# Masks by rows with a place each, output-projection parts issued one by one, a third weight tile in the masks' place, and later loads in order

## The chip, the cores and the metric

The kernel runs on one core of one Trainium2 chip. Its five engines each run their own instruction stream and meet at semaphores: PE multiplies matrices, ACT does activations and copies, DVE and POOL do elementwise work, SP issues the DMAs. The metric is the device time of one execution in microseconds; each kernel is run several times and the median counts.

## The reference, cut to what matters

One inference step of a two-layer trunk of width 1024, over a prompt of 1024 tokens and a sample of 64 tokens that share the weights. Layer 0 is sparse attention (an indexer picks 256 keys for each query) beside a short gated convolution; layer 1 is a spatial gating unit. Only what layer 0 does between the choice of keys and its output projection matters here:

```python
rel = relu(einsum('bqhd,bsd->bqhs', qi, ki))
score = einsum('bqh,bqhs->bqs', wi, rel)
score = where(adm, score, -inf)                 # causal by chunks of 64
top_val, top_idx = lax.top_k(score, topk)       # ties go to the lower index
logits = einsum('bqgrd,bqkgd->bqgrk', q, k[top_idx], ...) * HEAD_DIM ** -0.5
p = softmax(where(valid, logits, -inf))
o = einsum('bqgrk,bqkgd->bqgrd', p, v[top_idx])
a_out = o * silu(ga)
out = concatenate([a_out, b_out], axis=-1) @ w_out
x = x + gate * out
```

Instead of gathering, the kernel finds a threshold for each query by a binary search and adds a mask to dense logits.

## The kernel before

Prompt and sample are one token axis of 1088 columns. Numbers are float32, and each operand of a large product is held as two parts, a rounded high part and the exact rest; a product is three matmuls: high x high, rest x high, high x rest. The parts of the activations are `ah` and `al`, those of a weight tile `w_hi` (ACT, L249) and `w_lo` (POOL, or DVE where asked, L250). A weight tile `w_raw` is 128 x 1024 numbers; two places alternate for it, and each of `w_hi` and `w_lo` has two as well. `split` (L288) makes high and rest of any tile: a copy on ACT (L289) and a subtraction on DVE or POOL (L290).

A framework scheduler sets the order of instructions on each engine by their dependencies and the order of the code; on PE the attention part keeps the order of the code. All DMAs go through SP's queue in its order. A tile of a pool that takes the place of another waits until the other is done with.

In layer 0, after the scores S, `topk` leaves a threshold T for each query. Then:

- **Masks.** Seven blocks j of 128 queries have key widths of 384, 512, 640, 768, 896, 1024 and 576. `mask(j)` does one block: the sign of score less threshold with its sum (ACT, L619), its square with its sum (ACT, L620, written to `cum`), two small steps that count the ties to admit (`cv`, DVE, L621 and L622), a running count over the row (DVE, L623), the choice (DVE, L624) and a scaling to the mask's size (ACT, L625). `cum` is one tile with two halves, used in turn by even and odd blocks. Masks are written to the tile `bias`. All `mask(j)` are issued ahead of the first 360 steps of filler work (`BEFORE`), and the parts of the queries and of the sample's keys (`queries`, `sample_keys`: `st`, `kc`, `qs`) behind those.
- **Attention.** `attend` walks through slots. A slot transposes probabilities (`p_ps`, split into `pth` on ACT and `ptl` on DVE), issues logits some slots ahead (PE `logit_ps` L662; DVE L663 adds the mask and takes the minimum; ACT L667 exponentiates; POOL L669 normalises), and multiplies probabilities by values (`av` L706). Between these PE takes filler matmuls from the generator `side`: first projection tiles (`pj`, L258 and L275), then, once the convolution and the first heads of the first token piece are there (`halved`), the first two output-projection tiles for that piece (`early_out`, L1089).
- **Output projection.** Tokens are in three pieces of 448, 384 and 256 (`OUT_CHUNKS`), inputs in eight blocks k of 128 (`OUT_KTS`), outputs in eight weight tiles. `out_split(c, k)` makes `ah` and `al` of piece c and block k out of `q` (attention, already multiplied by its gate at L1025) or `bo` (convolution). `early_out` issues those of piece 0 in its steps, with `al` on POOL except for k = 3. Those of pieces 1 and 2 are written behind `attend` and are bound by nothing but their inputs, so the scheduler places them as soon as these are ready. The weight tiles from the third on have places in a pool opened after the attention's, with `w_lo` of the third on POOL and of the others on DVE. The residual x is loaded in three pieces: the first on its own, the other two behind the last weight load (`issue_after`). Then x is updated at L1110 out of the product `op`.

The other two names of the prediction: `corner` is a constant part of the masks, and `ln_g`, `ln_b` are the norm weights of layer 1.

Of the kernel before, what the change touches and what calls it, by code (L numbers as in the profile page):

```python
# [9 lines left out]
F32 = mybir.dt.float32  # L10
# [7 lines left out]
P = 128  # L18
# [17 lines left out]
NCH = 3  # L36
# [67 lines left out]
class Trunk:  # L104
# [130 lines left out]
    def weights(self, src, lo_eng="pool", pair=None):  # L235
# [6 lines left out]
        return self.weight_parts(raw, lo_eng, pair or (pool, n))  # L242

    def weight_parts(self, raw, lo_eng, place):
        nc = self.nc
        pool, n = place
        hi = pool.tile([P, KT, P], F32R, tag=f"whi{n}", name="w_hi")
        lo = pool.tile([P, KT, P], F32R, tag=f"wlo{n}", name="w_lo")
# [39 lines left out]
    def split(self, hi, lo, src, lo_eng=None):  # L288
        self.nc.scalar.activation(hi, src, AF.Copy)  # L289
        (lo_eng or self.nc.vector).tensor_sub(lo, src, hi)  # L290
# [315 lines left out]
    def mask(self, j):  # L606
# [5 lines left out]
        n = SW[j]  # L612
        sl = self.S[:, SOFF[j]:SOFF[j] + n]
        bi = self.bias[:, SOFF[j]:SOFF[j] + n]
        p = slice(COL[j], COL[j] + 1)
        c = self.cv[:, p]
        cum = self.cum[:, j % 2 * SEQ:j % 2 * SEQ + n]
        sums = self.small.tile([P, 4], F32, tag="sm", name="sums", bufs=8)
        A.activation(bi, sl, AF.Sign, scale=self.sgn[:, p], bias=self.T[:, p], accum_out=sums[:, 0:1])  # L619
        A.activation(cum, bi, AF.Square, accum_out=sums[:, 1:2])  # L620
        V.tensor_add(c, sums[:, 0:1], sums[:, 1:2])  # L621
        V.tensor_scalar(c, c, 0.5, self.kneg[:, p], op0=OP.mult, op1=OP.add)  # L622
        V.tensor_tensor_scan(cum, self.ones.to_broadcast([P, n]), cum, c, OP.add, OP.subtract)  # L623
        V.scalar_tensor_tensor(bi, cum, 0.0, bi, op0=OP.is_gt, op1=OP.is_gt)  # L624
        A.activation(bi, bi, AF.Copy, scale=MASK)  # L625
# [18 lines left out]
    def logits(self, it, e, c):  # L644
# [21 lines left out]
        if c == k - 1:  # L666
            nc.scalar.activation(p, p, AF.Exp, scale=-1.0, bias=st[:, c:c + 1], accum_out=st[:, 2:3])  # L667
            nc.vector.reciprocal(st[:, 3:4], st[:, 2:3])  # L668
            nc.gpsimd.tensor_scalar(p, p, st[:, 3:4], 0.5, op0=OP.mult, op1=OP.mult)  # L669
# [23 lines left out]
    def weighted(self, pool, it, js, parts):  # L693
# [92 lines left out]
    def attend(self, pool, through, half):  # L786
# [73 lines left out]
    def layer0(self):  # L860
# [41 lines left out]
        with ExitStack() as es:  # L902
# [5 lines left out]
            self.bias = mid.tile([P, STOT], BF, name="bias")  # L908
            self.corner = mid.tile([P, 256], BF, name="corner")
# [65 lines left out]
            with self.pool("attn", "right") as ap:  # L975
                self.at = 0

                self.cum = ap.tile([P, 2 * TC], BF, tag="ga", name="cum")
# [61 lines left out]

                self.halved = False
                self.p, self.both, self.live, self.last = {}, {}, {}, False
                self.side = chain(tiles(), self.early_out(fetch))
                self.tags = ["pj", "pj", "lg", "lg", "lg"]
                with self.tc.manual_schedule(engines={mybir.EngineType.PE}):
                    for j in range(NSB):
                        self.mask(j)
# [3 lines left out]
                    self.queries(ap, 0)  # L1051
                    self.sample_keys(ap)
# [15 lines left out]
    def out_split(self, c, k):  # L1068
# [291 lines left out]
```

## Time and profile before

| | |
|---|---|
| median of 3 runs (lowest to highest) | 1142.4 us (1141.48 to 1142.86) |
| the profiled execution, whole | 1143.23 us |
| its span (first to last instruction) | 1141.5 us |
| mean granted clock of PE | 0.981 |
| masks begin to end (ACT 381.83, last mask copy) | 381.8 to 418.8 us |
| attention ends (last `av`) | 620.5 us |

In rows of the trace the columns are start, duration, engine, line, operation, written tile <- read tiles, shape; "x5" are five in a row, and in square brackets stand the idle time before and what ended it. In groups the columns are the busy time, the mean in ns, and the idle time before with its releasers. In the tables by stretches they are the stretch, its length, then for PE, PE's weight loads, DVE, ACT and POOL the busy time and the number of instructions, then PE's granted clock (1.00 is full), the share of the DMA engines and GB/s.

### The profile page before, as it was taken

The page shows a single profiled execution, that of the slowest core. Times are in us where ns is not written, and L with a number is a line of the kernel's source. Part 1 is how long each engine was busy: PE and PEld are TensorE (multiplying, and loading weights), DVE is VectorE, ACT ScalarE, POOL GpSimd, SP SyncE. Part 2 cuts the span into 40 slices and gives each one's busy share as a digit, 9 for nine tenths or more (in the row PEclk, how much of TensorE's full clock was granted, in tenths as well). Part 3 has the DMA queues.
Part 4 walks back from the last instruction along what each step waited for, and adds up shares of the span by engine and source line. Part 5 has one row for each costly group of instructions (what it writes and reads, how often), then busy time and mean ns, then how long its engine had stood idle before and what let it go on. Part 6 is the DMA issues. An engine that isn't in the chain of part 4 may idle for free.

```text
span 1141.5 us, 18854 instructions
## 1 busy us (share of the span) xinstructions
PE 1088.0 (95%) x7255; PEld 1049.4 (92%) x7255; DVE 659.1 (58%) x1618; ACT 524.0 (46%) x1002; POOL 465.6 (41%) x482
## 2 busy tenths in 40 slices
PE   4899999999999979999978999999999999999996
PEld 4789689999999979999967899999999999999996
DVE  5711799998888697777785344311194064247134
ACT  5232586856766766676764223512212111235111
POOL 2633223466557555464491246422133201154222
PEclk9999999999999989999978899999999999999999
DMA  9745501211001110000002601011112101131012
GB/s 362 313 158 198 201 29 56 77 56 38 27 31 38 57 38 19 20 20 20 20 19 77 228 1 38 1 57 37 46 57 74 44 31 37 38 111 38 1 66 92
DMA packets 25786, 81.84 MB, mean 72 GB/s; under 512 B 3040, under 2 KB 9440, under 8 KB 23264
## 3 DMA queue, kind: packets, MB, share of 16 engines
q1 hardware_dynamic: 25696, 80.63, 19.9%
q8 instruction: 57, 0.93, 0.3%
q14 instruction: 33, 0.27, 0.1%
HBM read 74.50 MB, written 6.12 MB: 71 GB/s over the span
## 4 chain that ended last, share of the span: by engine, by line
PE 82%; DVE 8%; ACT 4%; DMA 2%; issue 2%; POOL 2%; SPq 0%; POOLq 0%; DVEq 0%; ACTq 0%
PE pj L258 41%; PE op L258 15%; PE pj L275 8%; PE av L706 3%; PE logit_ps L662 3%; PE p_ps L688 3%; PE ada_ps L164 1%; PE sgu_ps L1170 1%; PE score_ps L440 1%; PE first L331 1%; DVE cum L623 1%; DVE al L290 1%; POOL hf L342 1%; PE score_ps L441 1%; DMA w_raw<-in_w 1%
## 5 line engine op out<-in xcount | busy, mean ns | idle before, releaser
L258 PE MATMUL pj<-ah,w_hi 128*128 128x364 f32 (+1 forms) x984 | 326.0, 331 | 1.0 <-ACT w_hi L249 1.0
L258 PE MATMUL pj<-al,w_hi 128*128 128x364 f32 (+1 forms) x984 | 323.8, 329 | 0.0
L258 PE MATMUL pj<-ah,w_lo 128*128 128x364 f32 (+1 forms) x984 | 323.0, 329 | 0.0
L250 POOL TENSOR_TENSOR w_lo<-w_raw,w_hi 128x1024 fp32r<-128x1024 f32 x64 | 159.2, 2489 | 337.9 <-ACT w_hi L249 324.2
L258 PEld LDWEIGHTS pj<-ah,w_hi 128*128 128x128 f32 x984 | 185.0, 188 | 2.0 <-ACT w_hi L249 1.3
L258 PEld LDWEIGHTS pj<-ah,w_lo 128*128 128x128 f32 x984 | 184.9, 188 | 0.3 <-issue 0.2
L258 PEld LDWEIGHTS pj<-al,w_hi 128*128 128x128 f32 x984 | 185.1, 188 | 0.0
L258 PE MATMUL op<-ah,w_hi 128*128 128x384 f32 (+2 forms) x368 | 122.2, 332 | 4.3 <-ACT w_hi L249 4.3
L249 ACT ACTIVATE w_hi<-w_raw 128x1024 fp32r<-128x1024 f32 x69 | 73.0, 1059 | 114.3 <-PE pj L258 86.9
L258 PE MATMUL op<-ah,w_lo 128*128 128x384 f32 (+2 forms) x368 | 120.6, 330 | 1.5 <-DVE w_lo L250 1.5
L258 PE MATMUL op<-al,w_hi 128*128 128x384 f32 (+2 forms) x368 | 121.5, 330 | 0.3 <-DVE al L290 0.3
L542 DVE TENSOR_SCALAR_CACHE_REDUCE junk<-S,cand 128x512 bf16<-128x512 f32 (+5 forms) x142 | 119.0, 838 | 1.9
L275 PE MATMUL pj<-ah,w_lo 128*128 128x364 f32 (+1 forms) x288 | 95.8, 332 | 0.9 <-POOL w_lo L250 0.9
L275 PE MATMUL pj<-ah,w_hi 128*128 128x364 f32 (+1 forms) x288 | 95.5, 332 | 0.0
L275 PE MATMUL pj<-al,w_hi 128*128 128x364 f32 (+1 forms) x288 | 95.3, 331 | 0.0
L1110 DVE SCALAR_TENSOR_TENSOR x<-op,mod,x 128x192 f32<-128x192 f32 (+2 forms) x64 | 30.3, 497 | 105.8 <-PE op L258 102.6
L569 ACT ACTIVATE junk<-S,cand 128x896 bf16<-128x896 f32 (+2 forms) x78 | 77.8, 998 | 29.1 <-DVE m L572 25.4
L669 POOL TENSOR_SCALAR S<-S,sm 128x128 f32<-128x128 f32 (+8 forms) x68 | 51.9, 767 | 72.3 <-DVE sm L668 59.7
L258 PEld LDWEIGHTS op<-ah,w_hi 128*128 128x128 f32 x368 | 70.5, 192 | 6.9 <-ACT w_hi L249 5.0
L1118 POOL TENSOR_TENSOR acc<-acc,sq 128x448 f32<-128x448 f32 (+2 forms) x40 | 39.5, 988 | 88.5 <-ACT sq L1116 87.8
L258 PEld LDWEIGHTS op<-ah,w_lo 128*128 128x128 f32 x368 | 70.2, 191 | 4.1 <-DVE w_lo L250 2.1
L258 PEld LDWEIGHTS op<-al,w_hi 128*128 128x128 f32 x368 | 70.4, 191 | 2.6 <-DVE al L290 0.7
(248 smaller groups left out, 2033.8 us busy)
## 6 DMA issues: line engine op xcount, KB each, us to landing
w_raw<-in_w SPq DMA_DIRECT2D x53, 512.0 KB, 3.5
ada<-in_ada_w SPq DMA_DIRECT2D x19, 1024.0 KB, 9.1
w_raw<-in_wo SPq DMA_DIRECT2D x16, 512.0 KB, 3.5
x<-in_x SPq DMA_DIRECT2D x8, 544.0 KB, 6.6
bo<-in_ada_w SPq DMA_DIRECT2D x4, 1024.0 KB, 6.9
x<-in_x SPq DMA_DIRECT2D x1, 1792.0 KB, 8.7
out_y<-x SPq DMA_DIRECT2D x1, 1792.0 KB, 6.6
x<-in_x SPq DMA_DIRECT2D x1, 1536.0 KB, 9.8
```

Source lines behind the costliest of these rows:

```text
L249: nc.scalar.activation(hi, raw, AF.Copy)
L250: (nc.gpsimd if lo_eng == "pool" else nc.vector).tensor_sub(lo, raw, hi)
L258: last = self.nc.tensor.matmul(ps, wt[:, kt, :], at[:, kt, c0:c1], start=n == 0, stop=n == len(mms) - 1)
L275: self.nc.tensor.matmul(ps, wt[:, kt, :], at[:, kt, a:b], start=kt == 0 and i == 0, stop=kt == KT - 1 and i == 2)
L542: V.tensor_scalar(junks[0][:, 0:SW[j]], self.S[:, span(j)], thr, 0.0, op0=OP.is_lt, op1=OP.add, accum_out=col(cv, j))
L569: nc.scalar.activation(junks[1][:, 0:SW[j]], self.S[:, span(j)], AF.Sign, scale=-1.0, bias=col(cand, j), accum_out=col(cv, j))
L662: nc.tensor.matmul(pt[:, 0:w], lhs, keys[i][:, t // 2, s], start=i == 0, stop=i == 1)
L669: nc.gpsimd.tensor_scalar(p, p, st[:, 3:4], 0.5, op0=OP.mult, op1=OP.mult)
L688: nc.tensor.transpose(pt[0:r, o:o + P], p[:, j * P:j * P + r], self.ident)
L706: nc.tensor.matmul(av[:, 0:m], self.vs[0:r, vbase + j, t // 2, :], part[0:r, x:x + m], start=j == 0 and i == 0, stop=(j + 1) * P >= n and ...
L1110: nc.vector.scalar_tensor_tensor(x[:, t, a:b], ps[:, a:b], self.mod[l][:, 16 + t, j:j + 1], x[:, t, a:b], op0=OP.mult, op1=OP.add)
L1118: nc.gpsimd.tensor_add(acc, acc, sq)
```

## The change

1. `masks(pool)` takes the place of `mask(j)`: first sign and square for all seven blocks, then the DVE steps for all seven, then all seven scalings. Each block has a place of its own for `cum`, in memory of tiles that the attention uses later (`ga`, `ptl`, `pth`). The parts of the queries and of the sample's keys are written ahead of the masks.
2. The subtractions of `out_split` for piece 0 move from POOL to DVE. The splits of pieces 1 and 2 (k other than 3) become a generator, `late`: each slot of `attend`, once `halved`, issues one, on POOL, behind the last split's copy and the last normalisation. What is left of them and k = 3 stand behind `attend`.
3. A new `third` loads the third output weight tile when the last logits are issued, and writes its parts into the place of `bias`, which for that lives in a pool of its own (`held`). Its subtraction is on POOL.
4. The other output weight tiles subtract on DVE; the first piece of x is loaded behind the fourth tile, the others behind the last, `ln_g` and `ln_b` behind those. The rest of the output projection is held behind the last `av`.

```diff
+    def masks(self, pool):
...
+        wide = pool.tile([P, 2 * TC], BF, tag="ga", name="cum")
+        cums = [wide[:, 0:SEQ], wide[:, SEQ:2 * SEQ]] + [
+            pool.tile([P, 2 * 512], BF, tag=t, name="cum", bufs=3) for t in ("ptl", "ptl", "ptl", "pth", "pth")]
+        rows = []
+        for j in range(NSB):
...
+            A.activation(bi, sl, AF.Sign, scale=self.sgn[:, p], bias=self.T[:, p], accum_out=sums[:, 0:1])
+            A.activation(cum, bi, AF.Square, accum_out=sums[:, 1:2])
+            rows.append((n, bi, cum, p, sums))
+        for n, bi, cum, p, sums in rows:
+            c = self.cv[:, p]
+            V.tensor_add(c, sums[:, 0:1], sums[:, 1:2])
+            V.tensor_scalar(c, c, 0.5, self.kneg[:, p], op0=OP.mult, op1=OP.add)
+            V.tensor_tensor_scan(cum, self.ones.to_broadcast([P, n]), cum, c, OP.add, OP.subtract)
+            V.scalar_tensor_tensor(bi, cum, 0.0, bi, op0=OP.is_gt, op1=OP.is_gt)
+        for n, bi, *_ in rows:
+            A.activation(bi, bi, AF.Copy, scale=MASK)
...
                 waiting.append((it, js, self.transposes(pool, it, js)))
+                if self.halved:
+
+                    with self.tc.issue_after(self.lasthi), self.tc.issue_after(self.lastnorm):
+                        next(self.late, None)
...
+                if not ahead:
+                    self.third()
...
+                def third():
...
+                    place = self.held.tile([P, STOT // 2], F32R, tag="bias", name="w_2")[:, 0:2 * KT * P]
+                    self.wo.append(self.weights(self.i["wo0"][2], place=place.rearrange("p (i k c) -> p i k c", i=2, k=KT)))
...
+                self.late = (self.out_split(c, k, nc.gpsimd) for c in range(1, NCH) for k in OUT_KTS if k != 3)
...
-                    for j in range(NSB):
-                        self.mask(j)
+                    self.queries(ap, 0)
+                    self.sample_keys(ap)
+                    self.masks(ap)
                     for _ in range(BEFORE):
                         next(self.side)
                     self.attending, self.tags = True, ["pj"]
-                    self.queries(ap, 0)
-                    self.sample_keys(ap)
                     self.attend(ap, through, half)
...
             for c in range(1, NCH):
-                for k in OUT_KTS:
-                    self.out_split(c, k)
+                self.out_split(c, 3)
...
-    def out_split(self, c, k):
+    def out_split(self, c, k, eng=None):
         s = slice(*OUT_CHUNKS[c])
-        self.split(self.ah[:, k, s], self.al[:, k, s], (self.q if k < 4 else self.bo)[:, k % 4, s],
-                   self.nc.gpsimd if k != 3 else None)
+        self.split(self.ah[:, k, s], self.al[:, k, s], (self.q if k < 4 else self.bo)[:, k % 4, s], eng)
...
-                ws = self.wo + [self.weights(self.i["wo0"][t], "dve" if t > 2 else "pool", (wp, t))
-                                for t in range(2, KT)]
-                with self.tc.issue_after(self.lastload):
-                    for c in range(1, NCH):
-                        self.load(self.xc[c], self.i["x"][:, :, slice(*OUT_CHUNKS[c])])
-                self.out_projection(0, ws, self.h1)
+                    for t in range(len(ws), KT):
+                        ws.append(self.weights(self.i["wo0"][t], "dve", (wp, t)))
+                        if t == 3:
+                            residual([0])
+                    residual(range(1, NCH))
+                    with self.tc.issue_after(self.lastav):
+                        self.out_projection(0, ws, self.h1)
```

How the instructions stand, first on ACT at the masks, from the last sign on. Before (`pj` is a filler product that the copy to `q` frees, `kc` the sample's keys):

```order
L619 ACTIVATE bias,sums<-S,T,sgn 128x576
L870 ACTIVATE q<-pj 128x360
L620 ACTIVATE cum,sums<-bias 128x384
L620 ACTIVATE cum,sums<-bias 128x512
L249 ACTIVATE w_hi<-w_raw 128x1024
L870 ACTIVATE q<-pj 128x364
L289 ACTIVATE kc_3875<-ckr 128x512
```

And after:

```order
L291 ACTIVATE kc_3878<-ckr 128x512
L624 ACTIVATE bias,sums<-S,T,sgn 128x576
L625 ACTIVATE cum,sums<-bias 128x384
L625 ACTIVATE cum,sums<-bias 128x512
L625 ACTIVATE cum,sums<-bias 128x640
L625 ACTIVATE cum,sums<-bias 128x768
L625 ACTIVATE cum,sums<-bias 128x896
L625 ACTIVATE cum,sums<-bias 128x1024
L885 ACTIVATE q<-pj 128x360
L625 ACTIVATE cum,sums<-bias 128x576
L251 ACTIVATE w_hi<-w_raw 128x1024
```

All squares now stand ahead of the next `w_hi`; the two copies of `kc` have moved in between the signs. On DVE the steps of all seven blocks now stand ahead of the first L663 (L672 in the new numbering), and on ACT the copies of later `pj` to `q` stand behind the last scaling.

Then POOL at the end of attention, from the long product on (`al` of 448 is piece 0, of 384 piece 1, of 256 piece 2). Before:

```order
L290 TENSOR_TENSOR al<-q,ah 128x384
L290 TENSOR_TENSOR al<-q,ah 128x256
L669 TENSOR_SCALAR S<-S,sm 128x1024
L290 TENSOR_TENSOR al<-bo,ah 128x384
L290 TENSOR_TENSOR al<-bo,ah 128x256
L290 TENSOR_TENSOR al<-bo,ah 128x384
L290 TENSOR_TENSOR al<-bo,ah 128x256
L290 TENSOR_TENSOR al<-bo,ah 128x384
L290 TENSOR_TENSOR al<-bo,ah 128x256
L250 TENSOR_TENSOR w_lo<-w_raw,w_hi 128x1024
L290 TENSOR_TENSOR al<-bo,ah 128x384
```

And after, over the same products and to the end of attention:

```order
L292 TENSOR_TENSOR al<-q,ah 128x256 x2
L678 TENSOR_SCALAR S<-S,sm 128x1024 x2
L252 TENSOR_TENSOR w_lo<-w_raw,w_hi 128x1024
L292 TENSOR_TENSOR al<-bo,ah 128x384
L678 TENSOR_SCALAR S<-S,sm 128x768
L292 TENSOR_TENSOR al<-bo,ah 128x384
L678 TENSOR_SCALAR S<-S,sm 128x768
L292 TENSOR_TENSOR al<-bo,ah 128x384 x2
L678 TENSOR_SCALAR S<-S,sm 128x896
L292 TENSOR_TENSOR al<-q,ah 128x384
L678 TENSOR_SCALAR S<-S,sm 128x896
L252 TENSOR_TENSOR w_6795<-w_raw,w_6795 128x1024
```

`w_lo` now stands behind two `al`, the others stand one or two between the normalisations (S), and the third tile's rest (`w_6795`) is the last row here. The seven `al` of piece 0 that stood on POOL stand on DVE.

Last SP's queue from the output weights on. Before:

```order
L126 DMA w_raw<-in_wo 128x1024 x4
L126 DMA lng<-in_ln_g 128x1024
L126 DMA lnb<-in_ln_b 128x1024
L126 DMA x_6971<-in_x 128x8x448
L126 DMA w_raw<-in_wo 128x1024 x3
L126 DMA x_6972<-in_x 128x8x384
L126 DMA x_6970<-in_x 128x8x256
L126 DMA w_raw<-in_wo 128x1024
```

And after:

```order
L126 DMA w_raw<-in_wo 128x1024 x5
L126 DMA x_6985<-in_x 128x8x448
L126 DMA w_raw<-in_wo 128x1024 x3
L126 DMA x_6986<-in_x 128x8x384
L126 DMA x_6984<-in_x 128x8x256
L126 DMA lng<-in_ln_g 128x1024
L126 DMA lnb<-in_ln_b 128x1024
```

One more weight load stands ahead of the first piece of x, and all eight ahead of its other pieces; `ln_g` and `ln_b` are last.

More of the change, by code (lines that the diff above doesn't have):

```diff
@@ L232, in rstd, with weights @@
         return pt[:, 0:w]
-    def weights(self, src, lo_eng="pool", pair=None):
+    def weights(self, src, lo_eng="pool", pair=None, place=None):
         nc = self.nc
@@ L241, in weights, with weight_parts @@
         self.load(raw, src)
-        return self.weight_parts(raw, lo_eng, pair or (pool, n))
-    def weight_parts(self, raw, lo_eng, place):
+        return self.weight_parts(raw, lo_eng, pair or (pool, n), place)
+    def weight_parts(self, raw, lo_eng, pair, place=None):
         nc = self.nc
-        pool, n = place
-        hi = pool.tile([P, KT, P], F32R, tag=f"whi{n}", name="w_hi")
-        lo = pool.tile([P, KT, P], F32R, tag=f"wlo{n}", name="w_lo")
+        if place is not None:
+            hi, lo = place[:, 0], place[:, 1]
+        else:
+            pool, n = pair
+            hi, lo = (pool.tile([P, KT, P], F32R, tag=f"w{x}{n}", name=f"w_{x}") for x in ("hi", "lo"))
         nc.scalar.activation(hi, raw, AF.Copy)
@@ L604, in topk @@
         V.scalar_tensor_tensor(T, T, -1.0, sgn, op0=OP.mult, op1=OP.mult)
-    def mask(self, j):
+    def masks(self, pool):
         nc = self.nc
         V, A = nc.vector, nc.scalar
[L612 to L625, printed above, removed]
+        wide = pool.tile([P, 2 * TC], BF, tag="ga", name="cum")
[3 more added lines that the diff above has]
+        for j in range(NSB):
+            n = SW[j]
+            sl, bi, cum = self.S[:, SOFF[j]:SOFF[j] + n], self.bias[:, SOFF[j]:SOFF[j] + n], cums[j][:, 0:n]
+            p = slice(COL[j], COL[j] + 1)
+            sums = self.small.tile([P, 4], F32, tag="sm", name="sums", bufs=8)
+            A.activation(bi, sl, AF.Sign, scale=self.sgn[:, p], bias=self.T[:, p], accum_out=sums[:, 0:1])
[9 more added lines that the diff above has]
+            A.activation(bi, bi, AF.Copy, scale=MASK)
     def sample(self, it):
@@ L705, in weighted @@
             for i, part in enumerate(parts):
-                nc.tensor.matmul(av[:, 0:m], self.vs[0:r, vbase + j, t // 2, :], part[0:r, x:x + m],
-                                 start=j == 0 and i == 0, stop=(j + 1) * P >= n and i == 1)
+                self.lastav = nc.tensor.matmul(av[:, 0:m], self.vs[0:r, vbase + j, t // 2, :], part[0:r, x:x + m],
+                                               start=j == 0 and i == 0, stop=(j + 1) * P >= n and i == 1).ins
         if (js[-1] + 1) * P >= n:
@@ L907, in layer0 @@
             mid = es.enter_context(self.pool("mid", "right"))
-            self.bias = mid.tile([P, STOT], BF, name="bias")
-            self.corner = mid.tile([P, 256], BF, name="corner")
+            self.bias = self.held.tile([P, STOT], BF, tag="bias", name="bias")
+            self.corner = self.held.tile([P, 256], BF, name="corner")
             self.q = self.qi = mid.tile([P, 4, TC], F32, name="q")
@@ L976, in layer0 @@
                 self.at = 0
-                self.cum = ap.tile([P, 2 * TC], BF, tag="ga", name="cum")
+                ap.tile([P, TC], F32, tag="ga", name="place")
                 self.kc = [ap.tile([P, 2 * NS], F32R, tag=f"kc{i}", name=f"kc{i}").rearrange("p (g n) -> p g n", g=2)
@@ L1056, in layer0 @@
                 self.attending = False
+            for _ in self.late:
+                pass
             for c in range(1, NCH):
-                for k in OUT_KTS:
-                    self.out_split(c, k)
+                self.out_split(c, 3)
     def spans(self, c):
@@ L1196, in layer1 @@
                     self.lng, self.lnb = lp.tile([P, D], F32, name="lng"), lp.tile([P, D], F32, name="lnb")
-                    self.load(self.lng, i["ln_g"].partition_broadcast(P))
-                    self.load(self.lnb, i["ln_b"].partition_broadcast(P))
+                    with self.tc.issue_after(self.lastload):
+                        self.load(self.lng, i["ln_g"].partition_broadcast(P))
+                        self.load(self.lnb, i["ln_b"].partition_broadcast(P))
                     def gelu(t):
```

33 lines of the change are left out of this document (21 added, 12 removed).

## The prediction

> **What bounds the kernel.** I read the page first: who is busy, and for how much of the span.
>
> ```profile
> span 1141.5 us, 18854 instructions
> PE 1088.0 (95%) x7255; PEld 1049.4 (92%) x7255; DVE 659.1 (58%) x1618; ACT 524.0 (46%) x1002; POOL 465.6 (41%) x482
> ```
>
> PE (the matmuls) is the bound. The change leaves PE's matmuls as they are in number, so it can win only what PE waits (span less busy: 53.5 us) and what PE loses at a low clock. The table by stretches shows where this lies near the change; PEclk is the third number from the end. The second row is all of the stretch in which POOL never stops.
>
> ```profile
> 409.20:416.00 6.80, 3.84 (x14) 3.84 (x15) 6.73 (x13) 5.27 (x9) 2.46 (x2) 0.50 0.11 28
> 577.45:596.92 19.47, 12.84 (x67) 11.49 (x65) 15.05 (x22) 11.65 (x27) 19.47 (x21) 0.74 0.03 9
> 586.70:603.70 17.00, 11.14 (x38) 9.75 (x39) 14.23 (x18) 5.68 (x14) 12.04 (x13) 0.50 0.10 32
> 603.70:620.50 16.80, 16.80 (x115) 16.06 (x113) 9.23 (x22) 7.75 (x15) 2.04 (x2) 1.00 0.01 1
> 624.20:634.40 10.20, 8.06 (x20) 6.35 (x21) 3.83 (x3) 3.73 (x5) 3.31 (x2) 0.50 0.84 312
> ```
>
> PE's waits (from whom: us in total, times, longest), first the larger of two at the masks (365 to 425 us; the other, 0.91, is in a row further down), then those of the end of attention (570 to 660 us):
>
> ```profile
> PE logit_ps L662 <- DVE sm L663: 6.7, 2, 6.3
> ```
>
> ```profile
> PE op L258 <- ACT w_hi L249: 4.3, 1, 4.3
> PE op L1089 <- POOL w_lo L250: 3.8, 1, 3.8
> PE op L1089 <- DVE ga L1001: 2.7, 1, 2.7
> PE op L258 <- DVE w_lo L250: 1.5, 1, 1.5
> PE logit_ps L662 <- DVE sm L663: 1.3, 1, 1.3
> ```
>
> So the end of attention holds 13.6 us of waits. At clock 0.50 PE's busy time is twice what the work needs, so half of 11.14 and of 8.06, 9.6 us, is lost besides. **That is 23.2 us in reach there**, and 7.6 + 1.9 (half of 3.84) = 9.5 us at the masks.
>
> On the clock: it stood at 0.50 from 586.70 on, although the wait before (until 587.42) is only 2.70 us long. [...]
>
> **Why PE waits at the end of attention.**
>
> ```profile
> 587.97 5.01 POOL L290 TENSOR_TENSOR al<-bo,ah 128x384 fp32r<-128x384 f32 x6
> 592.91 2.36 POOL L250 TENSOR_TENSOR w_lo<-w_raw,w_hi 128x1024 fp32r<-128x1024 f32 x1
> 588.91 8.49 DVE L1025 TENSOR_TENSOR q<-q,ga 128x448 f32<-128x448 f32 x1
> 585.39 1.05 ACT L249 ACTIVATE w_hi<-w_raw 128x1024 fp32r<-128x1024 f32 x1
> L289 ACT ACTIVATE ah<-bo 128x384 fp32r<-128x384 f32 (+2 forms) x9 | 3.8, 475 | 0.0
> ```
>
> POOL subtracts the exact parts of all three token pieces as one train, of which the first row is a piece. The w_lo that PE needs has its w_hi at 586.44 but starts at 592.91, behind the train: 6.5 us. A DVE product is held 8.49 us with no semaphore, and ends when the train ends. The ga wait is of the same family: ACT has nine ah copies (3.8 us) and more of them on q in its queue ahead of w_hi and ga.
>
> [...]
>
> **The change at the end of attention.** The fourteen splits of pieces 1 and 2 (k other than 3) leave the train and come one per slot; the seven subtractions of piece 0 go from POOL to DVE. So w_lo follows its w_hi at once (3.8 gone), ga comes some 3 us or more earlier on ACT (2.7 gone), and the product finds gaps. What is late next is DVE:
>
> ```profile
> 575.00:600.00 25.00, 17.04 (x87) 15.08 (x86) 19.52 (x33) 15.16 (x35) 22.83 (x24) 0.73 0.07 22
> L290 DVE TENSOR_TENSOR al<-q,ah 128x384 fp32r<-128x384 f32 x1 | 0.6, 559 | 0.3 <-ACT ah L289 0.3
> ```
>
> An al of 448 on DVE is 0.65 us by the 384 row (559 ns x 448/384). Seven more are 4.6 us, put ahead of logit evacuations (L663) and probability parts (ptl) for which PE waits. DVE has room: 19.52 busy, of which some 7.8 is the held product. I let half of 4.6 reach PE: 2.3 (bounds 0 and 4.6). A late split's POOL half (5.01/6, 0.84 each) can hold DVE too, now singly: 1.5, a fifth of the 7.8 (2.7 + 3.8 + 1.3) seen under the train. Logits whose L663 comes late anyway: 2.0, the 1.33 seen and half as much again.
>
> The last wait, 4.3 us, comes after the final av (L706), which ends at 624.86 - 4.31 = 620.55:
>
> ```profile
> 624.86 0.74 PE L258 MATMUL op<-ah,w_hi 128*128 128x448 f32 x1 [4.31 <-ACT w_hi L249]
> 619.27 0.36 PE L1089 MATMUL op<-al,w_hi 128*128 128x448 f32 x1
> 619.07 0.37 PE L1089 MATMUL op<-ah,w_hi 128*128 128x448 f32 x1
> 623.75 2.01 ACT L249 ACTIVATE w_hi<-w_raw 128x1024 fp32r<-128x1024 f32 x2 [0.66 <-DVE al L290]
> 625.79 2.55 DVE L250 TENSOR_TENSOR w_lo<-w_raw,w_hi 128x1024 fp32r<-128x1024 f32 x1 [2.07 <-ACT w_hi L249]
> 634.47 2.47 DVE L250 TENSOR_TENSOR w_lo<-w_raw,w_hi 128x1024 fp32r<-128x1024 f32 x2 [1.70 <-ACT w_hi L249]
> ```
>
> With the third tile made early in the masks' place, 24 matmuls at 0.20 us (619.27 less 619.07) fill 620.5 to 625.4. By then w_hi of the fourth tile is there (623.75 + 1.0 = 624.8), and its w_lo at 626.0 (2.47/2 each), since POOL no longer subtracts the third tile there, which stretched the 2.55 row. I leave 0.2. The third tile itself costs ACT 1.05 and POOL 2.4 us in a stretch in which both are mostly idle (603.70 to 620.50: 7.75 and 2.04 busy of 16.80).
>
> The moved loads: x for piece 0 now stands behind five weight loads.
>
> ```profile
> x<-in_x SPq DMA_DIRECT2D x1, 1792.0 KB, 8.7
> 412.18 1.28 ACT L667 ACT_TABLE_LOAD   x1
> ```
>
> It takes 8.7 us from issue to landing. It needs memory of the attention tiles, free at about 621, so it arrives near 630, and tiles 2 and 3 fill PE until 625.4 + 4.9 = 630.3: 0.5 for it (0 to 3). The ln_g and ln_b loads, now last, are used only in layer 1: 0. At the start an additional table load stands on ACT and two memsets come earlier on POOL; a table load takes 1.28 in the second row, and the start hangs on the loads of x: 0, at most 1.3.
>
> PE's waits after: 2.3 + 1.5 + 2.0 + 0.2 + 0.5 = 6.5. For the clock I keep two stretches of 3.4 us (the 17.0 and 10.2 us at clock 0.50 are five and three such pieces) at half: 3.4. **Gain: 23.2 - 9.9 = 13.3.** At best 20 (3.2 left); at worst 4 (the first three waits and their 5.6 stay, the new al cost all 4.6, and the end gives 4.3 + 1.5 + 4.0 = 9.8 less 1.5 for the load).
>
> **The change at the masks.**
>
> ```profile
> 388.46 0.45 ACT L870 ACTIVATE q<-pj 128x360 f32<-128x360 f32 x1
> L620 ACT ACTIVATE cum<-bias 128x384 bf16<-128x384 bf16 (+6 forms) x7 | 5.3, 763 | 0.0
> L289 ACT ACTIVATE kc<-ckr 128x512 fp32r<-128x512 f32 x2 | 1.3, 630 | 0.0
> 400.99 3.84 POOL L250 TENSOR_TENSOR w_lo<-w_raw,w_hi 128x1024 fp32r<-128x1024 f32 x1
> 393.80 0.44 PE L275 MATMUL pj<-ah,w_lo 128*128 128x364 f32 x1 [0.91 <-POOL w_lo L250]
> ```
>
> On ACT two kc copies and all seven Squares now stand ahead of w_hi (before, two Squares): the signs end at 388.46, so it starts at 388.5 + 1.3 + 0.4 + 5.3 = 395.5 and ends at 396.6. Its w_lo takes 2.4 (592.91) to 3.84 us, so PE's matmul of 393.80 comes at 399.0 to 400.4: a wait of some 6.5 us for 0.91. It hides in the later one of 6.28 us:
>
> ```profile
> 412.16 0.69 PE L662 MATMUL logit_ps<-kp,st 128*128 128x128 f32 x2 [6.28 <-DVE sm L663]
> L623 DVE TENSOR_TENSOR_SCAN cum<-ones,cv,cum 128x384 bf16<-128x384 f32 (+6 forms) x7 | 13.4, 1913 | 0.2
> L624 DVE SCALAR_TENSOR_TENSOR bias<-cum,bias 128x384 bf16<-128x384 bf16 (+6 forms) x7 | 9.0, 1287 | 0.1
> L621 DVE TENSOR_TENSOR cv<-sums 128x1 f32<-128x1 f32 x7 | 4.3, 621 | 7.7 <-ACT cum L620 7.7
> L622 DVE TENSOR_SCALAR cv<-cv,kneg 128x1 f32<-128x1 f32 x7 | 1.5, 211 | 0.2
> 389.45:418.11 28.66, 21.33 (x116) 20.27 (x114) 28.13 (x36) 19.55 (x43) 17.09 (x10) 0.88 0.16 56
> 418.14 0.69 ACT L625 ACTIVATE bias<-bias 128x576 bf16<-128x576 bf16 x1
> ```
>
> What sets PE's return is now the whole mask chain: all DVE rows stand ahead of the first L663, and the q copies that free PE's banks stand behind the last mask copy on ACT. The chain is 13.4 + 9.0 + 4.3 + 1.5 = 28.2 us. Part of that is waiting for POOL, at most POOL's 17.09 busy beside it; L621, as small as L622, takes 0.62 for 0.21 in the mean, 2.9 us in seven, and the scans and products hold more. I put 8 to POOL, about half of 17.09, so 20.2 free. After, the chain starts at 388.5 + 1.3 + 0.5 (the first Square) = 390.3 and ends between 410.5 and 418.5; POOL's kc subtractions come ahead of it now, two w_lo and qs stay within, so I take the middle, 414.5, and 0.69 + 0.45 for the last copies: PE returns at 415.6, not 412.16. **Cost: 3 us**, the new wait being spent within it (-1 where the chain is free, +8 at 418.5 with one more stretch at half clock, 1.7). The clock loss of 1.9 stays.
>
> **Sum.** 1143.2 us, the profiled execution's own time (its span and 1.7 around it, which stay), - 13.3 + 3 = 1132.9. The median of the runs shown, 1142.4, is 0.8 below that execution: **1132.1**.
>
> **Rivals.**
> - The mask chain loses nothing (qs and w_lo find gaps; -1) and DVE keeps up at the end (gain 17): about 1124. For it: the cums no longer wait for each other. Against: w_hi is late for certain.
> - Slower: the masks. If every POOL instruction in the chain holds DVE for its whole length, as the 8.49 row shows is possible, the chain's free 20.2 us grow by 17.1 to end at 427.6; PE returns at 428.7, 16.6 late, and one more stretch runs at half clock (1.7): 1142.4 - 13.3 + 18.3 = 1147.4. It decides from a return at about 424, where the cost reaches the 13 us. Against: before, about half of POOL's time was passed on, and kc now comes earlier.
> - Half the gain: the 8.49 us hold is not the train's doing, or it moves to the seven new al on DVE, and the first three waits come back in part: tail gain 7, 1142.4 - 7 + 3 = 1138.4.
> - The paced splits don't open the queue (POOL still full when w_lo is due) so the gain is the 4 of the worst case, and the masks cost 5: 1142.4 - 4 + 5 = 1143.4, no change. Against: the fourteen splits, 11.8 us of POOL, are spread to 620, over a stretch with 2.04 us of POOL in 16.80.
>
> **Chances.** Forecast (1128 to 1136) 0.58; the first rival 0.08; half the gain 0.16; no change 0.08; slower 0.10. The range leaves out what lies past 1142 above and 1124.5 below. A measurement of this kernel tells about 0.2% from no change, 2.3 us: faster 0.82, same 0.08, slower 0.10.
>
> **What would show it.** Right: no POOL train, L1025 of 448 under 2 us, no w_hi wait after the last av, PE busy 620 to 630 at full clock; at the masks two waits of 4 to 6 us, one on w_hi. Wrong: PE waits on L663 or ptl of over 8 us in all from 570 to 620, a wait on x<-in_x that reaches PE near 630, or a return from the masks past 420.

## The result and the profile after

| | before | after |
|---|---|---|
| median of 4 runs (lowest to highest) | 1142.63 us (1141.48 to 1143.14) | 1126.57 us (1125.07 to 1127.61) |
| ratio, 95% interval | | 0.986 (0.9843 to 0.9877) |
| the profiled execution, and its span | 1143.23, 1141.5 us | 1125.07, 1123.4 us |

The kernel became 16 us faster; 10.3 was forecast. The time lies in the range (1124.5 to 1142), but 1.4 us under the narrower band (1128 to 1136) that had the chance of 0.58. The profile page of the changed kernel begins:

```profile
span 1123.4 us, 18847 instructions
PE 1080.6 (96%) x7255; PEld 1043.9 (93%) x7255; DVE 652.1 (58%) x1625; ACT 523.8 (47%) x1003; POOL 460.9 (41%) x475
```

PE is busy 7.4 us less with the same 7255 matmuls: that is time at half clock that is gone (mean granted clock 0.990, 0.981 before), the 9.6 us of the end of attention less some 2 us that this execution lost more at the masks (there the clock was 0.50 for 6.83 and for 3.41 us, before for 6.83). The other 10.7 of the 18.1 us are waits. To see where they went, three marks are of use that both programs have: POOL's product of 1088 before the last head group (the masks lie ahead of it), and DVE's two products behind the last value matmul (attention ends there). Rows of the trace, first of the kernel before, then of the changed one (L1025 has become L1040):

```profile
571.92 2.55 POOL L1025 TENSOR_TENSOR q<-q,ga 128x1088 f32<-128x1088 f32 x1 [0.29 <-DVE q L714]
621.68 0.89 DVE L1025 TENSOR_TENSOR q<-q,ga 128x384 f32<-128x384 f32 x2
```

```profile
572.68 2.55 POOL L1040 TENSOR_TENSOR q<-q,ga 128x1088 f32<-128x1088 f32 x1
612.98 0.89 DVE L1040 TENSOR_TENSOR q<-q,ga 128x384 f32<-128x384 f32 x2
```

| stretch | before | after | difference |
|---|---|---|---|
| start to first mark (masks in it) | 571.9 | 572.7 | +0.8 |
| first to second mark (end of attention) | 49.8 | 40.3 | -9.5 |
| second mark to the end | 519.8 | 510.4 | -9.4 |

PE's waits in the changed kernel, first 365 to 435 us, then 540 to 680 us:

```profile
PE pj L277 <- ACT w_hi L251: 3.7, 1, 3.7
PE pj L277 <- POOL w_lo L252: 1.9, 1, 1.9
PE logit_ps L671 <- ACT q L885: 1.2, 1, 1.2
PE logit_ps L671 <- DVE sm L672: 0.4, 1, 0.4
```

```profile
PE logit_ps L671 <- DVE sm L672: 1.6, 1, 1.6
PE p_ps L697 <- DVE ptl L292: 1.4, 2, 0.9
PE op L1113 <- DVE ga L1016: 0.7, 1, 0.7
```

At the end of attention 3.7 us of waits are left of 13.6, each under 1.7, and none comes after the last `av`. By stretches, with the clock third from the end of a row:

```profile
570.00:612.00 42.00, 38.30 (x255) 36.02 (x254) 32.35 (x82) 31.43 (x67) 27.99 (x25) 1.00 0.08 26
612.00:640.00 28.00, 28.00 (x139) 25.61 (x138) 13.74 (x18) 9.84 (x15) 7.55 (x6) 1.00 0.74 266
```

PE doesn't stop for 28 us from the third weight tile on, and the clock stays full in both. POOL is now busy 28 of 42 us. Before, it had no pause for 25 us; the prediction's stretch of 19.47 us, there called all of it, is only the later part:

```profile
571.92:596.92 25.00, 18.37 (x104) 16.74 (x102) 20.00 (x35) 17.13 (x40) 25.00 (x24) 0.79 0.03 7
```

The two operations that had stood behind its train:

```profile
587.54 2.39 POOL L252 TENSOR_TENSOR w_lo<-w_raw,w_hi 128x1024 fp32r<-128x1024 f32 x1 [0.68 <-ACT w_hi L251]
589.39 1.02 DVE L1040 TENSOR_TENSOR q<-q,ga 128x448 f32<-128x448 f32 x1
```

w_lo starts when its w_hi is there, and the product takes 1.02 us instead of 8.49.

### The profile page after: what moved, and what is told of

It reads as the page before. It is cut to its first block, busy times and chain, and to the rows that moved or that the text cites. A ratio compares the mean times of both kernels' runs of the same rounds, so it can differ in the third digit from the quotient of the medians.

```text
span 1123.4 us, 18847 instructions
## 1 busy us (share of the span) xinstructions
PE 1080.6 (96%) x7255; PEld 1043.9 (93%) x7255; DVE 652.1 (58%) x1625; ACT 523.8 (47%) x1003; POOL 460.9 (41%) x475
## 4 chain that ended last, share of the span: by engine, by line
PE 84%; DVE 6%; ACT 3%; DMA 3%; issue 2%; POOL 2%; SPq 0%; POOLq 0%; DVEq 0%; ACTq 0%
PE pj L260 42%; PE op L260 15%; PE pj L277 9%; PE av L715 3%; PE logit_ps L671 3%; PE p_ps L697 3%; PE ada_ps L164 1%; PE sgu_ps L1194 1%; PE score_ps L442 1%; PE first L333 1%; DVE cum L631 1%; DVE al L292 1%; DMA x<-in_x 1%; POOL hf L344 1%; PE score_ps L443 1%
## 5 line engine op out<-in xcount | busy, mean ns | idle before, releaser
L252 POOL TENSOR_TENSOR w_lo<-w_raw,w_hi 128x1024 fp32r<-128x1024 f32 x63 | 156.9, 2491 | 321.8 <-ACT w_hi L251 314.9
L260 PE MATMUL op<-al,w_hi 128*128 128x256 f32 (+2 forms) x344 | 112.0, 326 | 0.6 <-DVE al L292 0.6
L260 PE MATMUL op<-ah,w_hi 128*128 128x256 f32 (+2 forms) x344 | 112.3, 327 | 0.0
L260 PE MATMUL op<-ah,w_lo 128*128 128x256 f32 (+2 forms) x344 | 111.6, 326 | 0.0
L260 PEld LDWEIGHTS op<-al,w_hi 128*128 128x128 f32 x344 | 64.9, 189 | 2.7 <-DVE al L292 1.0
L1140 ACT ACTIVATE sq<-x 128x448 f32<-128x448 f32 (+2 forms) x42 | 21.2, 506 | 97.1 <-DVE x L1134 93.6
L260 PEld LDWEIGHTS op<-ah,w_hi 128*128 128x128 f32 x344 | 64.9, 189 | 1.7
```

The source lines that it names most:

```text
L252: (nc.gpsimd if lo_eng == "pool" else nc.vector).tensor_sub(lo, raw, hi)
L260: last = self.nc.tensor.matmul(ps, wt[:, kt, :], at[:, kt, c0:c1], start=n == 0, stop=n == len(mms) - 1)
```

## The experiments

Every run of a line was timed beside the kernel before on the same chip. "First stretch", "attention" and "rest" are the three stretches above, from the one profiled execution. "From first sign" is the part of the first stretch from the first sign of the masks on (381.83 us in the kernel before, where the part is 190.1): what lies ahead of it differs between these executions by up to 2.7 us, which no edit here explains.

| run | median us | ratio to before (95%) | first stretch | from first sign | attention | rest |
|---|---|---|---|---|---|---|
| changed kernel | 1126.57 | 0.986 (0.9843 to 0.9877) | 572.7 | 191.3 | 40.3 | 510.4 |
| changed kernel, again | 1125.52 | 0.9847 (0.9833 to 0.9861) | 571.9 | 190.1 | 41.8 | 510.1 |
| e1 masks as before | 1125.12 | 0.984 (0.9825 to 0.9854) | 571.8 | 190.2 | 41.8 | 510.0 |
| e2 free later splits | 1130.43 | 0.9879 (0.986 to 0.9897) | 573.5 | 191.3 | 45.8 | 511.0 |
| e3 first piece on POOL | 1122.75 | 0.9825 (0.981 to 0.9839) | 572.3 | 191.1 | 38.6 | 510.2 |
| e8 both of these | 1133.32 | 0.9901 (0.9879 to 0.9923) | 574.8 | 191.1 | 47.3 | 510.5 |
| e11 half the train | 1131.05 | 0.9886 (0.9857 to 0.9914) | 575.0 | 191.1 | 45.3 | 510.5 |
| e4 no early third tile | 1130.94 | 0.989 (0.9875 to 0.9905) | 571.7 | 190.1 | 41.1 | 516.7 |
| e10 the same, its rest on POOL | 1134.66 | 0.9922 (0.9907 to 0.9937) | 572.4 | 190.1 | 41.1 | 519.3 |
| e5 w_hi ahead of the squares | 1125.37 | 0.9846 (0.9829 to 0.9863) | 573.2 | 189.3 | 41.8 | 510.8 |
| e6 qs behind the masks | 1128.22 | 0.9869 (0.9852 to 0.9886) | 573.8 | 192.2 | 40.3 | 510.6 |
| e7 e5 and e6 | 1122.76 | 0.9822 (0.9808 to 0.9835) | 570.3 | 188.5 | 40.3 | 510.6 |
| e9 e3 and e7 | 1120.44 | 0.9795 (0.978 to 0.981) | 570.5 | 188.4 | 38.6 | 509.7 |

The kernel before was 1142.69 beside the repeat and e5 to e7, 1143.71 beside e1 to e4, 1143.47 beside e8 to e10, and 1142.5 beside e11.

### The changed kernel again

> The changed kernel once more, as the measure for the three runs beside it: median near 1126.6, span near 1123.4.

1125.52 us, span 1123.8. The attention stretch is 1.5 us longer than in the first profile and the masks 1.1 us shorter, with the same waits; why, is told under the unexpected.

### e1: the masks as before

```diff
-                    self.queries(ap, 0)
-                    self.sample_keys(ap)
-                    self.masks(ap)
+                    for j in range(NSB):
+                        self.mask(j)
                     for _ in range(BEFORE):
                         next(self.side)
                     self.attending, self.tags = True, ["pj"]
+                    self.queries(ap, 0)
+                    self.sample_keys(ap)
...
```

`mask(j)` and its `cum` of two halves are those of the kernel before (not shown).

> The changed kernel with the masks as before (block by block, two halves of one cum tile, queries and sample keys behind). My theory: the new order of the masks cost 1 to 2 us (the stretch from the first sign to the middle of attention is 1.2 us longer in the changed kernel, 0.76 + 0.4), so this is 1.2 us faster, span about 1122.2, and PE's waits there are again 0.9 and 6.3. Rival: a place for each cum is worth something by itself; then this is 2 us or more slower than the changed kernel (span over 1125.4).

PE's waits there are those of before again, 0.9 and 6.3 us. The median is 1.4 us under the changed kernel's first measurement and 0.4 under its second, with overlapping intervals. From the first sign to the first mark the old masks take 190.1 and 190.2 us (the kernel before and e1). Of eight executions with the new ones (the changed kernel twice, e2, e3, e4, e8, e10, e11) three take 190.1, and five 191.1 to 191.3. In three of these five (the changed kernel, e2, e3) the granted clock from 365 to 425 us is 0.91 in the mean, for 0.94 in the repeat and e4: one stretch of 3.4 us more at half clock (two of the eight are looked into under the unexpected). So the masks by rows gain nothing, and cost nothing or 1 us, as it happens. The span, 1123.7, is not the 1122.2 expected.

### e2: later splits free

```diff
-                if self.halved:
-
-                    with self.tc.issue_after(self.lasthi), self.tc.issue_after(self.lastnorm):
-                        next(self.late, None)
```

> The changed kernel with the splits of pieces 1 and 2 no longer paced one to a slot but free to stand wherever they are ready; the first piece's subtractions stay on DVE. My theory: the POOL train returns (14 subtractions, 11.8 us), w_lo waits behind it and the long product on DVE is held until its end, so of the 9.5 us that attention ends earlier 6 to 9 are lost: span 1129.4 to 1132.4, product of 448 over 5 us, a PE wait on w_lo of 2 us or more, half clock again. Rival: taking seven subtractions off POOL was what opened the queue; then this is within 2 us of the changed kernel.

4 to 5 us slower by the medians, less than the 6 to 9 expected and more than the rival's 2 (the profiled execution, the slowest of the four, has a span in the expected range, 1130.3). A part of the train was back (`al` in sixes and fours), w_lo stood behind it with a PE wait of 2.1 us, and two stretches ran at half clock (the mean is 0.59 in 584.05 to 587.46 and in 597.70 to 601.12 us); but the product of 448 was not held, against what I expected:

```profile
590.03 3.37 POOL L292 TENSOR_TENSOR al<-bo,ah 128x384 fp32r<-128x384 f32 x4
593.35 2.77 POOL L252 TENSOR_TENSOR w_lo<-w_raw,w_hi 128x1024 fp32r<-128x1024 f32 x1
593.28 0.61 DVE L1036 TENSOR_TENSOR q<-q,ga 128x448 f32<-128x448 f32 x1
```

Its turn on DVE came (593.28) only when the four `al` ended. POOL still had work without a pause until 598.16, and the product got in all the same; w_lo took 2.77 us instead of 2.37.

### e3: the first piece's subtractions on POOL again

```diff
-                self.out_split(0, OUT_KTS[n])
+                self.out_split(0, OUT_KTS[n], self.nc.gpsimd if OUT_KTS[n] != 3 else None)
```

> The changed kernel with the first piece's seven subtractions back on POOL, the later splits still paced. My theory: POOL has room for them before 584 (about 1 us each where 11.8 us of late splits stood), w_lo stays in time, so it is within 2 us of the changed kernel, span 1121.4 to 1125.4; DVE's waits of PE (1.6 and 1.4 us) may even go. Rival: the move to DVE carries a good part of the gain; then 3 us or more slower.

3 us faster than the changed kernel, a little beyond my range for "no change". PE's waits on L672 are gone, and on `ptl` 0.7 us are left of 1.4:

```profile
PE p_ps L697 <- DVE ptl L292: 0.7, 2, 0.5
PE op L1113 <- DVE ga L1016: 0.6, 1, 0.6
```

The attention stretch is 1.7 us shorter than in the first profile of the changed kernel, where these waits cost no clock (1.00 from 570 to 612 us), and 3.2 shorter than in its repeat, where they did (0.50 from 579.91 to 583.33). So moving these seven to DVE, ahead of what PE waits for, cost the change 2 to 4 us.

### e8: both edits of the splits undone

The edits of e2 and e3 together; POOL's rows then stand as before the change.

> Both edits of the splits undone in the changed kernel: the first piece's subtractions on POOL and the later splits free, so that POOL's rows stand as before the change, while the masks and the third tile stay as changed. My theory after the two single runs (free splits alone cost 5 us, the first piece on POOL alone gained 3): they are not a sum; with both, the train again fills POOL, the product of 448 on DVE is held to its end (over 5 us, where it took 0.61 with the first piece on DVE), and attention ends 8 to 9.5 us later than in the changed kernel: span 1131.4 to 1133. Rival: the two effects add up, 5 - 3 = 2 us slower, span about 1125.5, product under 2 us.

As expected (span 1132.6): the two effects don't add, 5 and -3 by themselves, 7 to 8 us slower together. The train and the hold return within 0.02 us of each row:

```profile
590.86 5.01 POOL L292 TENSOR_TENSOR al<-bo,ah 128x384 fp32r<-128x384 f32 x6
595.79 2.38 POOL L252 TENSOR_TENSOR w_lo<-w_raw,w_hi 128x1024 fp32r<-128x1024 f32 x1
598.09 1.73 POOL L292 TENSOR_TENSOR al<-bo,ah 128x384 fp32r<-128x384 f32 x2
591.80 8.50 DVE L1036 TENSOR_TENSOR q<-q,ga 128x448 f32<-128x448 f32 x1
```

The product (8.50, before 8.49) ends at 600.30, 0.48 us behind POOL's last `al` (599.82). PE's waits are back as well:

```profile
PE op L1109 <- POOL w_lo L252: 5.1, 1, 5.1
PE op L1109 <- DVE ga L1012: 2.7, 1, 2.7
```

These are 7.8 us, as much as before the change. Against e3, from which this run differs by the pacing alone, the stretch is 8.7 us longer (47.3 against 38.6). So the train was the cause of most of what PE lost before the last `av`. The 2.5 us still missing to the 49.8 of before fit the clock: 10.2 us ran at half here, 17.1 there (mean granted clock of the whole run 0.986, 0.981 before). No wait of PE in this run is for the held product or for what stands behind it on DVE; what PE pays for is w_lo, and ga.

### e11: half the train

```diff
-                self.late = (self.out_split(c, k, nc.gpsimd) for c in range(1, NCH) for k in OUT_KTS if k != 3)
+                self.late = (self.out_split(c, k, nc.gpsimd) for c in (2,) for k in OUT_KTS if k != 3)
...
+            for k in OUT_KTS:
+                if k != 3:
+                    self.out_split(1, k, nc.gpsimd)
...
```

The edit of e3 stands in this run too.

> As the run with the whole train back, but only the splits of piece 1 stand free; those of piece 2 come one to a slot. Behind the second normalisation of 1024 POOL's train is three al of 384, w_lo, an al of 384 and one of 256, some 7 us instead of 9.1. My theory: the product of 448 is held to the end of whatever POOL has ready without a gap, so it takes 4 to 6 us instead of 8.50, and the stretch from the product of 1088 to the end of attention lies between that with both edits of the splits kept as paced (38.6) and that of the whole train (47.3): 41 to 44, span 1124 to 1128. [...]

Both sizes came out above my ranges: product 6.52 us, stretch 45.3 (span 1130.8). The product was held over six POOL instructions, the longest of them (w_lo) 2.37 us:

```profile
588.95 2.96 POOL L292 TENSOR_TENSOR al<-bo,ah 128x384 fp32r<-128x384 f32 x3
591.84 2.37 POOL L252 TENSOR_TENSOR w_lo<-w_raw,w_hi 128x1024 fp32r<-128x1024 f32 x1
594.14 1.72 POOL L292 TENSOR_TENSOR al<-bo,ah 128x384 fp32r<-128x384 f32 x2
596.52 0.90 POOL L678 TENSOR_SCALAR S<-S,sm 128x768 f32<-128x768 f32 x1 [0.66 <-DVE sm L677]
589.82 6.52 DVE L1040 TENSOR_TENSOR q<-q,ga 128x448 f32<-128x448 f32 x1
```

The hold ends (596.34) 0.48 us behind the place where POOL first had to wait for something (595.86, idle 0.66). A shorter train, a shorter hold.

### e4 and e10: no early third tile

```diff
-                if not ahead:
-                    self.third()
```

> The changed kernel without the early third weight tile: it is made after attention in the later pool, its rest on DVE. My theory: PE waits again some 4.3 us for w_hi after the last av and 1 to 2 us for w_lo, and runs at half clock for 6 to 10 us: 8 to 10 us slower, span 1131.4 to 1133.4. Rival: only the wait returns and the clock stays full: 4 to 6 us slower.

The rest is 6.3 us longer (516.7 against 510.4). By the medians the run is 4.4 us slower than the changed kernel and 5.4 than its repeat, which is the rival's size, but the rival's reason is out, for the clock did not stay full:

```profile
614.53:621.36 6.83, 6.22 (x16) 5.21 (x17) 2.67 (x4) 1.51 (x2) 0.00 (x0) 0.50 0.90 326
```

PE waits 3.5 us for w_hi, nothing for w_lo, and half of 6.22 is lost at the low clock: together 6.6. Without the wait for w_lo my own sum was too large. e10 is e4 with the third tile's rest on POOL:

```diff
-                        ws.append(self.weights(self.i["wo0"][t], "dve", (wp, t)))
+                        ws.append(self.weights(self.i["wo0"][t], "dve" if t > 2 else "pool", (wp, t)))
```

> No early third tile, and its rest on POOL beside the fourth's on DVE, as before the change. My theory: the two subtractions hold each other up again (2.55 us for one on DVE), PE waits for w_lo besides w_hi, and of the 9.4 us by which the stretch after attention had become shorter the last 3 are lost: 2 to 4 us slower than the run without the early tile alone (from the last product of attention to the end 519 to 520 us, against 516.7). Rival: the order of the loads makes these 3 us; then the same as that run.

519.3, against 519.8 before the change, with the wait for w_lo back:

```profile
PE op L260 <- ACT w_hi L251: 3.5, 1, 3.5
PE op L260 <- DVE w_lo L252: 1.5, 1, 1.5
```

So of the 9.4 us in the rest, 6.3 are the early tile, and 2.6 that POOL and DVE no longer subtract two weight tiles at once (a w_lo on DVE took 2.49 us in e10, where the third tile's is on POOL; two in a row took 2.36 in e4). What else the change moved there (the loads, the order behind the last `av`) is at most the 0.5 left over; it was not tried by itself.

### e5, e6, e7: what sets the return from the masks

e5 writes 225 filler steps ahead of the masks, e6 holds `qs` behind the last scaling, e7 does both:

```diff
+                    for _ in range(225):
+                        next(self.side)
                     self.masks(ap)
-                    for _ in range(BEFORE):
+                    for _ in range(225, BEFORE):
                         next(self.side)
```

```diff
...
-        for t in range(2):
-            self.both_parts(pool, t)
+        with self.tc.issue_after(self.lastmask):
+            for t in range(2):
+                self.both_parts(pool, t)
```

> The changed kernel with the first 225 filler steps written ahead of the masks, so that ACT makes the next tile's w_hi behind the first sign instead of behind all squares (PE's order is the same). My theory: the waits on w_hi and w_lo (3.7 + 1.9 us) go, but PE then waits for the end of the mask chain on DVE (412.1), so that the later wait grows from 1.2 to about 6 and it returns at about the same time: gain 0 to 2 us (only the half clock behind the first wait). Rival: the wait on w_hi is what costs; gain 5 us or more.

No gain in the median, within the expected 0 to 2: the waits for w_hi and w_lo are gone and turn up as one of 8.0 us for DVE. From the first sign the profile is 0.8 us shorter than the repeat's.

```profile
414.76 0.69 PE L671 MATMUL logit_ps<-kp,st 128*128 128x128 f32 x2 [8.02 <-DVE sm L672]
```

> The changed kernel with the sample's query parts (qs, four POOL subtractions that took 6.4 us beside the masks) behind the last mask. My theory: DVE's mask chain loses what POOL held up, 3 to 5 us, and ends near 408; PE finishes its tile only at 412.1, so it gains the later wait alone, about 1 us. Rival: POOL's subtractions do not hold DVE; then the chain ends as before, and the time is the same or longer for the later qs.

Here my theory fell. First the changed kernel (its repeat), then e6:

```profile
402.86 6.41 POOL L760 TENSOR_TENSOR qs<-q,qs 64x64 fp32r<-64x64 f32 x4
411.72 0.76 DVE L632 SCALAR_TENSOR_TENSOR bias<-cum,bias 128x576 bf16<-128x576 bf16 x1
```

```profile
413.15 1.48 POOL L759 TENSOR_TENSOR qs<-q,qs 64x64 fp32r<-64x64 f32 x4 [10.49 <-ACT qs L758]
411.38 0.76 DVE L632 SCALAR_TENSOR_TENSOR bias<-cum,bias 128x576 bf16<-128x576 bf16 x1
```

`qs` takes 1.48 us by itself and 6.41 beside the masks, and the chain on DVE ends at the same time with or without it (0.34 us earlier, of which 0.1 is that its signs begin earlier). There DVE held POOL, not POOL DVE. The run is 2.7 us slower by the median. From the first sign its profile is 2.0 us longer than the repeat's: some 0.8 is that `qs` now stands on ACT ahead of the copies that free PE's banks, and behind that longer wait came a stretch at half clock (415.85 to 419.26 us, where a filler matmul took 0.51 us, for 0.33 behind it) that the repeat doesn't have. What the median has beyond that is open.

> Both edits. My theory: only together do they move PE's return, since the tile's late weights and the mask chain end within 1 us of each other: PE returns 4 to 5 us earlier and the half clock is less, gain 4 to 6 us, span about 1118. Rival: one of the two edits alone already has all of the gain of both.

2.8 us faster than the repeat of the changed kernel, a bit over half of what I expected, though neither edit gains by itself in the median. The first logits return at 407.66, but the next wait until 412.40:

```profile
407.66 0.44 PE L670 MATMUL logit_ps<-kp,st 128*128 128x128 f32 x2 [3.05 <-ACT q L885]
412.40 0.80 PE L670 MATMUL logit_ps<-kp,st 128*128 128x256 f32 x2 [3.42 <-DVE sm L671]
```

since DVE's evacuation stands behind most of the masks still.

### e9: the edits that gained, together

> The changed kernel with the three edits that gained or help one another: first piece's subtractions on POOL (paced later splits), 225 filler steps ahead of the masks, qs behind the last mask. My theory: they lie in different stretches and add, 3 + 3 us: median near 1120, span about 1118.5. Rival: what the masks gain is lost again at the end of attention; then no better than the better of the two, 1122.7.

They add: 1120.44 us, with each stretch as long, within 0.1 us, as in the run that its edit comes from (188.4 from the first sign, 38.6 for attention). This is the best version found, 22 to 23 us below the kernel before and 5 to 6 below the changed one, both more than the intervals.

## Why the prediction was right, step by step

- **What bounds, and the reach.** Right. 18.9 of the 23.2 us held to be in reach at the end of attention were won, where 13.3 were forecast, and the masks moved little. The forecast was too small at the end and too large in the cost of the masks; the two errors point the same way, and only a wide range held the time.
- **The train.** Right as a mechanism, shown by e3 against e8 and by e11. (The train was longer than read: 25 us without a pause. And of the nine `ah` copies on ACT two stand behind w_hi and ga, at 586.69.) The term was mis-sized: before the last `av` I let 5.8 us of waits and 3.4 at half clock stay of 13.4, a gain of 4.2; it was 9.5. Two parts of it: the waits left were 3.7, and no stretch of half clock stayed (in the repeat one did, 1.7 us). That a POOL split holds DVE singly (1.5) did not show in PE's waits.
- **The seven subtractions on DVE.** The term of 2.3 (0 to 4.6) was right in size: e3 measures 1.7 in the stretch, 3.2 with the clock that it can cost. So the step is a loss within the change, which the pacing more than pays for; only with free splits does it seem to pay (e2 against e8: 3 us in the medians, 1.5 in the stretch, and the intervals overlap).
- **Behind the last `av`.** Forecast 9.1 (9.8 less 0.2 and 0.5), measured 9.4; the early tile and the end of the double subtraction both show in e4 and e10. The load of x did reach DVE as a wait of 4.15 us, but PE had tiles to go on with, so the 0.5 was not needed:

```profile
621.90 2.46 DVE L1134 SCALAR_TENSOR_TENSOR x<-op,mod,x 128x448 f32<-128x448 f32 x4 [4.15 <-DMA x<-in_x]
```

- **The masks.** The new wait for w_hi and w_lo came (5.6 us, forecast 6.5) and was spent within the old one, as said; the return came at 413.26, not 415.6, and the whole cost 0 to 1 us, not 3. The step that was off is the length of the chain: I added group sums whose rows overlap. In the changed kernel the chain took 389.7 to 412.1, 22.4 us. Two rows are held beside w_lo, by 4.0 us together (such rows take 1.82 and 0.15 us elsewhere), and none by `qs`; the 4 us put to POOL, the middle of 0 to 8, were met, but what is left, 18.4, is less than the 20.2 I had, and it began 0.6 earlier:

```profile
395.87 6.56 POOL L252 TENSOR_TENSOR w_lo<-w_raw,w_hi 128x1024 fp32r<-128x1024 f32 x2 [6.17 <-ACT w_hi L251]
396.36 3.91 DVE L631 TENSOR_TENSOR_SCAN cum<-ones,cv,cum 128x768 bf16<-128x768 f32 x1
400.41 2.03 DVE L629 TENSOR_TENSOR cv<-sums 128x1 f32<-128x1 f32 x1
```

 "Two waits of 4 to 6 us" was wrong for the second, which is 1.6 in all.
- **The rivals.** The first, given 0.08, came nearer than its chance: its 1124 is 2.6 us from the median, the forecast 5.5. At the end its gain of 17 was passed, and `qs` found room, as it says; but w_lo held DVE, and the masks did not gain. The slower one, the mask chain held by all of POOL's work, is out: the chain ended at 412.1, not 427.6, and e6 shows that one of its two large items, `qs`, didn't hold DVE. That the hold is not the train's doing is out by e8 and e11.

## What to carry to other kernels

An engine that is busy for 41% of the span, as POOL is here, can still set the end: look for stretches in which it never pauses, and for what stands behind them in its own queue and on the engine that it holds up. Here work that was ready early was best issued one piece at a time between pieces that others wait for; but moving it to another engine ahead of that engine's own urgent work was a loss, although that engine had room. And two edits at one place need not add: where two chains end within a microsecond, it may take both edits together to move anything (e5, e6, e7), and where both feed one queue, each alone may hide the other (e2, e3, e8).

## What the runs showed of the hardware that was not expected

**In three runs the hold lasted as long as POOL had ready work.** The product of 448 was held 8.49 us before the change, 8.50 in e8 and 6.52 in e11, over six to eight POOL instructions, and ended each time 0.48 us behind the place where POOL first waited for something. In e3 it took 2.35 us, over the rest of w_lo and one `al`, and ended 0.49 behind them. So the end of one POOL instruction didn't let it in there. It isn't always so: in e2 (0.61 us) and in the changed kernel (1.02) the product got in behind one POOL instruction although POOL went on without a pause, and at the masks DVE held `qs` (6.41 us, 1.48 by itself). What decides is open.

**Half clock came behind steps in which PE was busy for up to 2.11 of 3.41 us.** In the profiles of the kernel before and of the changed one the stretches at half clock up to 640 us are 3.41, 6.83, 10.24 and 17.07 us long, which is one, two, three and five steps of 3.41 us. The rows show steps on that grid, with PE's busy time first behind the comma and the clock third from the end. The kernel before:

```profile
583.29:586.70 3.41, 1.38 (x7) 1.01 (x7) 1.64 (x5) 3.38 (x9) 3.41 (x5) 0.99 0.00 0
586.70:590.11 3.41, 2.69 (x11) 2.65 (x12) 2.64 (x5) 2.50 (x7) 3.41 (x5) 0.50 0.00 0
```

The changed kernel, first at the masks, then at the end of attention, then near the end of the run:

```profile
412.21:415.63 3.42, 1.98 (x12) 1.84 (x13) 0.60 (x4) 3.40 (x6) 0.98 (x1) 1.00 0.00 0
415.63:419.04 3.41, 3.41 (x14) 3.41 (x13) 1.36 (x8) 2.52 (x9) 2.61 (x5) 0.50 0.28 83
576.05:579.47 3.42, 2.24 (x14) 1.62 (x12) 3.38 (x10) 2.52 (x7) 1.75 (x2) 1.00 0.00 0
579.47:582.88 3.41, 2.09 (x13) 2.00 (x14) 3.37 (x8) 1.55 (x3) 0.53 (x2) 1.00 0.00 0
582.88:586.29 3.41, 3.41 (x26) 3.41 (x25) 3.27 (x13) 2.70 (x5) 2.00 (x3) 1.00 0.00 0
1111.95:1115.36 3.41, 2.11 (x18) 1.94 (x16) 0.77 (x3) 0.42 (x1) 0.33 (x1) 1.00 0.00 0
1115.36:1118.78 3.42, 0.69 (x2) 0.29 (x2) 1.79 (x5) 0.00 (x0) 0.71 (x1) 0.50 0.00 0
```

And its repeat, at the same two places:

```profile
412.66:416.08 3.42, 2.08 (x13) 1.94 (x14) 0.60 (x4) 3.40 (x6) 1.08 (x1) 1.00 0.00 0
416.08:419.49 3.41, 3.30 (x21) 2.95 (x20) 1.55 (x9) 2.42 (x9) 2.61 (x5) 1.00 0.30 90
576.50:579.91 3.41, 0.98 (x5) 0.47 (x4) 3.41 (x10) 1.27 (x4) 1.86 (x2) 1.00 0.00 0
579.91:583.33 3.42, 3.35 (x11) 3.16 (x12) 3.38 (x12) 1.66 (x3) 0.93 (x2) 0.50 0.00 0
```

In these rows a full-clock step with PE busy for 0.98, 1.38, 1.98 or 2.11 us is followed by half clock, one with 2.08, 2.09 or 2.24 is not, so the busy time alone doesn't tell which. The same two waits at the end of attention (0.9 and 1.6 us) fell into two steps in one execution and into one in the other, which is the 1.5 us by which their attention stretches differ. At the masks it is the other way round (1.98 against 2.08), which is the 1.1 us between the executions with the new masks. This may be a part of the spread of the times. A forecast of this size can't know on which side it falls.
